# Sliding-window copy: loads moved to GpSimd's queue, four half-batch stores first, and half of the last unit stored by plain transfers

## The chip, the cores and the metric

One core of a Trainium2 chip. The metric is device time in microseconds (us), a median over runs; the granted clock was 1.0 in every run. A profiled execution is one of these; its own clock (the "span") starts a little later and ends a little earlier than the time that is scored, by 1.7 us in all (195.64 against 193.9).

## The reference

For a batch of 16 images of 64 channels and 64 x 64 pixels, every window of 8 x 8 at stride 4 is copied out.

```python
n_h = (h - window_size) // stride + 1      # 15
n_w = (w - window_size) // stride + 1      # 15
for i in range(n_h):
    for j in range(n_w):
        result[:, i, j] = x[:, :, i*4 : i*4 + 8, j*4 : j*4 + 8]
```

16.78 MB come in and 58.98 MB go out: 3600 rows (16 x 15 x 15) of 16 KB. There is no arithmetic on the data.

## The kernel before

The input stays in on-chip memory (L). A partition holds 32 of the 64 channels (bit 6 of its number says which) and a quarter of the picture rows of one image. VectorE and ScalarE gather windows from L into one of four staging tiles G, a window of 16 KB per partition, and an indirect store on GpSimd's queue scatters the 128 rows. An index beyond the output makes the store skip that row: of the 33 x 128 rows of all stores 624 have such an index, and the trace has 3600 packets of 16 KB, one for each of the other rows.

```python
SMALL = 4
for y in range(NY):                 # two half-batches
    for q in range(HQ):             # four quarters of the picture
        load(nc.sync, 0, y, q, SMALL, CL)      # 8 partitions, channels 4..31
        load(nc.gpsimd, 0, y, q, 0, SMALL)     # the same partitions, channels 0..3
        load(nc.gpsimd, 1, y, q, 0, CL)        # 8 partitions from 64 up, channels 32..63
...
EARLY = 3
for t in range(NG):                 # zero what a half-batch store reads but doesn't write
    ...
        nc.vector.memset(G[t][p0 : p0 + QP, :, :, :], 0.0)
for y in range(NY):
    for j in range(EARLY):          # half-batch stores: 64 rows
        ...
        scatter(G[t % NG], (idx_y0, idx_y1)[y], j, 0)
units = [(j, s) for j in range(NW) for s in (0, 2) if s or j >= EARLY]
for j, s in units:
    if s == 0:                      # "plain" unit: 128 rows
        ...
        scatter(g, idx, j, s)
    else:                           # "cross" unit: 112 rows
        turn = j % 2
        fill(g, turn, s, j, 0, HP, (act, act))
        fill(g, 1 - turn, s + 1, j, 0, HP, (dve, dve))
        scatter(g, (idx_hi, idx_lo)[turn], j, s)
```

A cross unit has 16 rows that don't exist. With idx_hi they are skipped in partitions 64 to 127, with idx_lo in partitions 0 to 63.

Of the kernel before, what the change touches and what calls it, by code (L numbers as in the profile page):

```python
# [1 line left out]

# [4 lines left out]


@with_exitstack  # L10
def kernel(
    ctx: ExitStack,
    tc: tile.TileContext,
    x: bass.AP,
    window_size: int,
    stride: int,
    out: bass.AP,
):
    nc = tc.nc
    P = nc.NUM_PARTITIONS  # L20

    B, C, H, W = x.shape
    Bo, NH, NW, Co, WSo, WSo2 = out.shape
    WS = int(window_size)
    ST = int(stride)
    assert Bo == B and Co == C and WSo == WS and WSo2 == WS

    f32 = mybir.dt.float32
    i32 = mybir.dt.int32
    ALU = mybir.AluOpType  # L30
    CH = 2
    HQ = P // (B * CH)
    CL = C // CH
    RB = H // HQ
    NSLOT = RB // ST
    NWIN = NH * NW
    CFREE = C * WS * WS
    HP = P // CH
    YB = 8
    NY = B // YB  # L40
    QP = YB * HQ
    assert HQ == 4 and WS == 2 * ST and QP == 32 and NSLOT == 4

    lpool = ctx.enter_context(tc.tile_pool(name="lpool", bufs=1))
    ipool = ctx.enter_context(tc.tile_pool(name="ipool", bufs=1))
    gpool = ctx.enter_context(tc.tile_pool(name="gpool", bufs=1))


    L = lpool.tile([P, CL, RB, W], f32)
    x_v = x.rearrange("(y b) (ch cl) (hq r) w -> ch y hq b cl (r w)", y=NY, ch=CH, hq=HQ)  # L50


    SMALL = 4

    def load(eng, ch, y, q, c0, c1):
        p0 = ch * HP + y * QP + q
        eng.dma_start(out=L[p0 : p0 + QP - HQ + 1 : HQ, c0:c1, :, :], in_=x_v[ch, y, q, :, c0:c1, :])  # L57



    def itile(name):
        return ipool.tile([P, 1], i32, name=name)

    pi, tb, tq, tc_, th, idx, idx_y0, idx_y1, idx_lo, idx_hi = (
        itile(n) for n in ("pi", "tb", "tq", "tc", "th", "idx", "idx_y0", "idx_y1", "idx_lo", "idx_hi")
    )
    FAR = float(2 * B * NWIN)
    nc.gpsimd.iota(pi[:, :], pattern=[[0, 1]], base=0, channel_multiplier=1)  # L68

    def bits(d, shift, mask):  # L70
        nc.vector.tensor_scalar(out=d[:, :], in0=pi[:, :], scalar1=shift, scalar2=mask, op0=ALU.logical_shift_right, op1=ALU.bitwise_and)

    def mul(d, a, m):
        nc.vector.tensor_scalar(out=d[:, :], in0=a[:, :], scalar1=float(m), scalar2=None, op0=ALU.mult)  # L74

    def tt(d, a, b, op):
        nc.vector.tensor_tensor(out=d[:, :], in0=a[:, :], in1=b[:, :], op=op)  # L77

    bits(tb, 2, B - 1)
    bits(tq, 0, HQ - 1)  # L80
    bits(tc_, 6, 1)
    mul(tb, tb, NWIN)
    mul(th, tq, NSLOT * NW)
    tt(tb, tb, th, ALU.add)
    mul(th, tc_, NW)
    tt(idx, tb, th, ALU.add)

    bits(th, 5, 1)
    mul(th, th, FAR)
    tt(idx_y0, idx, th, ALU.add)  # L90
    nc.vector.tensor_scalar(out=th[:, :], in0=th[:, :], scalar1=-1.0, scalar2=FAR, op0=ALU.mult, op1=ALU.add)  # L91
    tt(idx_y1, idx, th, ALU.add)

    nc.vector.tensor_scalar(out=tq[:, :], in0=tq[:, :], scalar1=float(HQ - 1), scalar2=FAR, op0=ALU.is_equal, op1=ALU.mult)
    tt(th, tc_, tq, ALU.mult)
    tt(idx_hi, idx, th, ALU.add)
    nc.vector.tensor_scalar(out=tc_[:, :], in0=tc_[:, :], scalar1=-1.0, scalar2=1.0, op0=ALU.mult, op1=ALU.add)
    tt(th, tc_, tq, ALU.mult)
    tt(idx_lo, tb, th, ALU.add)
    mul(th, tc_, NW)  # L100
    tt(idx_lo, idx_lo, th, ALU.add)

    for y in range(NY):
        for q in range(HQ):
            load(nc.sync, 0, y, q, SMALL, CL)
            load(nc.gpsimd, 0, y, q, 0, SMALL)
            load(nc.gpsimd, 1, y, q, 0, CL)

    o_v = out.rearrange("b i j c r w -> (b i j) (c r w)")
    nxt = [min(p + 1, 31) for p in range(32)]  # L110
    NG = 4
    G = [gpool.tile([P, C, WS, WS], f32, name=f"G{n}") for n in range(NG)]

    def scatter(g, ix, j, s):
        st = nc.gpsimd.indirect_dma_start(  # L115
            out=o_v,
            out_offset=bass.IndirectOffsetOnAxis(ap=ix[:, 0:1], axis=0),
            in_=g.rearrange("p c r w -> p (c r w)"),
            in_offset=None,
            element_offset=(s * NW + j) * CFREE,  # L120
            bounds_check=B * NWIN - 1,
            oob_is_err=False,
        )
        tc.declare_no_dep(st.ins, group="stores", reason="each store writes rows of its own")
        tc.add_to_no_dep_group("stores", st.ins)

    def fill(g, half, s, j, lo, n, copies):

        d = slice(half * HP + lo, half * HP + lo + n)
        cols = slice(j * ST, j * ST + WS)  # L130
        for ch in (half, 1 - half):
            f = slice(ch * HP + lo, ch * HP + lo + n)
            cs = slice(ch * CL, (ch + 1) * CL)
            copy = copies[ch != half]
            if s < NSLOT - 1:
                copy(out=g[d, cs, :, :], in_=L[f, :, s * ST : s * ST + WS, cols])  # L136
            else:
                copy(out=g[d, cs, 0:ST, :], in_=L[f, :, s * ST : RB, cols])  # L138
                nc.vector.stream_shuffle(out=g[d, cs, ST:WS, :], in_=L[f, :, 0:ST, cols], mask=nxt)  # L139

    act, dve = nc.scalar.copy, nc.vector.tensor_copy



    EARLY = 3
    assert EARLY < NG
    for t in range(NG):
        for half in range(CH):
            p0 = half * HP + (QP if t < EARLY else 0)
            nc.vector.memset(G[t][p0 : p0 + QP, :, :, :], 0.0)  # L150
    t = 0
    for y in range(NY):
        for j in range(EARLY):
            for half in range(CH):
                copies = (dve, dve) if y and half and j == 1 else (act, dve)
                fill(G[t % NG], half, half, j, y * QP, QP, copies)
            scatter(G[t % NG], (idx_y0, idx_y1)[y], j, 0)
            t += 1

    units = [(j, s) for j in range(NW) for s in (0, 2) if s or j >= EARLY]  # L160
    for j, s in units:
        g = G[t % NG]
        t += 1
        if s == 0:
            for half in range(CH):
                fill(g, half, s + half, j, 0, HP, (act, dve))
            scatter(g, idx, j, s)
        else:

            turn = j % 2  # L170
            fill(g, turn, s, j, 0, HP, (act, act))
            fill(g, 1 - turn, s + 1, j, 0, HP, (dve, dve))
            scatter(g, (idx_hi, idx_lo)[turn], j, s)


# [1 line left out]
_INS = ['x', 'window_size', 'stride']  # L177
_OUTS = [((16, 15, 15, 64, 8, 8), 'float32')]

_NUMBERS = {'window_size': 8, 'stride': 4}  # L180


# [26 lines left out]
```

## Time and profile before

| | before |
|---|---|
| time | 195.66 us (195.56 to 195.69, 3 runs) |
| span in the profile | 193.9 us |
| VectorE, ScalarE, GpSimd busy | 68%, 64%, 27% |
| last load landed | 47.5 us |
| first store issued | 44.5 us |
| last store landed, engines of partitions 64 to 127 / 0 to 63 | 187.8 / 190.4 us |
| middle duration of a 16 KB packet of a store | 618 ns |

The rows to read first are the DMA digits of the page (tenths of busy time in each of 40 slices) and the GB/s below them. Landing times and packet durations come from the trace's records of semaphore steps (a semaphore is the counter on which engines wait for a transfer; each store on GpSimd's queue steps its own 16 times) and of packets (the pieces of a transfer, each with a start, a duration and a size in the trace: 4 KB in the loads, 16 KB in the stores, and many of 4 bytes). All times count from the start of the span.

### The profile page before, as it was taken

To read this page: it belongs to the slowest core of one execution; us is meant where nothing else is said; L and a number is where in the kernel's file an instruction comes from. 1 tells how busy PE (TensorE), PEld (TensorE's weight loads), DVE (VectorE), ACT (ScalarE), POOL (GpSimd) and SP (SyncE) were. 2 spreads that over 40 slices of the span, in tenths; PEclk is the share of its full clock that TensorE was granted. 3 is DMA by queue.
4 is the path that set the end of the run, shared out by engine and by line. 5 is a ranking of instruction groups with operands and counts; after the bars stand their busy time and mean duration, and the time that the engine had idled before them with its cause. 6 is when DMAs were issued, how large, how long until landed. Compare 5 with 4: busy or idle time off the path is not lost.

```text
span 193.9 us, 478 instructions
## 1 busy us (share of the span) xinstructions
DVE 131.9 (68%) x156; ACT 123.5 (64%) x66; POOL 53.3 (27%) x54
## 2 busy tenths in 40 slices
DVE  6887778995999998766577657774777477643000
ACT  0000008960999999999779677977797779772000
POOL 7402211106463233231404211331323232311000
DMA  2999999999989999999999999999999999999980
GB/s 85 326 408 401 402 399 397 400 400 405 426 333 382 406 419 419 423 423 404 426 433 421 416 419 419 423 423 433 423 416 412 426 423 423 426 416 421 412 345 30
DMA packets 11476, 75.81 MB, mean 391 GB/s; under 512 B 3776, under 2 KB 3776, under 8 KB 7872
## 3 DMA queue, kind: packets, MB, share of 16 engines
q0 software_dynamic: 9616, 68.43, 85.9%
q1 hardware_dynamic: 1856, 7.34, 9.8%
q14 instruction: 4, 0.03, 0.0%
HBM read 16.78 MB, written 69.21 MB: 444 GB/s over the span
## 4 chain that ended last, share of the span: by engine, by line
DMA 66%; DVE 17%; issue 6%; POOL 2%; POOLq 1%; DVEq 0%; PEldq 0%
DMA out_dram<-G,idx 21%; DMA L<-in_x_dram 18%; DMA out_dram<-G,idx_hi 14%; DMA out_dram<-G,idx_lo 12%; DVE G L136 8%; DVE G L139 6%; DVE G L138 3%; POOL L L57 2%; POOLq L204 1%; DVEq L136 0%; POOL pi L68 0%; DVEq L138 0%; PEldq L204 0%
## 5 line engine op out<-in xcount | busy, mean ns | idle before, releaser
L136 ACT COPY G<-L 64x2048 f32<-64x2048 f32 (+1 forms) x65 | 122.2, 1896 | 22.5 <-DMA out_dram<-G,idx 9.9
L136 DVE COPY G<-L 64x2048 f32<-64x2048 f32 (+1 forms) x37 | 44.8, 1221 | 15.6 <-DMA out_dram<-G,idx 12.7
L139 DVE STREAM_SHUFFLE G<-L 64x1024 f32<-64x1024 f32 x30 | 38.3, 1275 | 0.0
L138 DVE COPY G<-L 64x1024 f32<-64x1024 f32 x30 | 20.7, 690 | 20.1 <-DMA out_dram<-G,idx_hi 13.3
L150 DVE MEMSET G<- 32x4096 f32 x8 | 27.8, 3472 | 7.9 <-issue 6.2
L115 POOL DMA_INDIRECT out_dram<-G,idx x12 | 12.4, 1030 | 33.3 <-ACT G L136 33.3
L115 POOL DMA_INDIRECT out_dram<-G,idx_hi x8 | 11.8, 1471 | 31.4 <-DVE G L139 17.8
L136 ACT ACT_TABLE_LOAD x1 | 1.3, 1283 | 29.6 <-DMA L<-in_x_dram 29.6
L57 POOL DMA_DIRECT2D L<-in_x_dram x16 | 9.8, 626 | 25.0 <-DMA L<-in_x_dram 24.4
L115 POOL DMA_INDIRECT out_dram<-G,idx_lo x7 | 9.7, 1390 | 20.5 <-ACT G L136 14.3
L115 POOL DMA_INDIRECT out_dram<-G,idx_y x6 | 9.3, 1547 | 13.7 <-DVE G L136 8.8
L77 DVE TENSOR_TENSOR th<-tc,tq 128x1 int32<-128x1 int32 x2 | 0.3, 159 | 0.1
L77 DVE CUSTOM_DVE_ANT_0 idx_y<-idx,th 128x2 uint16<-128x2 uint16 x2 | 0.3, 158 | 0.1
L74 DVE TENSOR_SCALAR th<-tc 128x1 int32<-128x1 int32 x2 | 0.3, 154 | 0.1
L68 POOL IOTA pi<- 128x1 int32 x1 | 0.1, 125 | 0.4 <-PEq L204 0.4
L139 DVE LOAD_MASK_SELECT G<-L x30 | 0.2, 6 | 0.0
L77 DVE CUSTOM_DVE_ANT_0 idx_hi<-idx,th 128x2 uint16<-128x2 uint16 x1 | 0.2, 159 | 0.0
L77 DVE CUSTOM_DVE_ANT_0 idx_lo<-tb,th 128x2 uint16<-128x2 uint16 x1 | 0.2, 159 | 0.0
L77 DVE CUSTOM_DVE_ANT_0 idx<-tb,th 128x2 uint16<-128x2 uint16 x1 | 0.2, 161 | 0.0
L77 DVE CUSTOM_DVE_ANT_0 idx_lo<-idx_lo,th 128x2 uint16<-128x2 uint16 x1 | 0.2, 158 | 0.0
L77 DVE CUSTOM_DVE_ANT_0 tb<-tb,th 128x2 uint16<-128x2 uint16 x1 | 0.2, 159 | 0.0
L91 DVE TENSOR_SCALAR th<-th 128x1 int32<-128x1 int32 x1 | 0.2, 153 | 0.0
(13 smaller groups left out, 1.7 us busy)
## 6 DMA issues: line engine op xcount, KB each, us to landing
L<-in_x_dram POOLq DMA_DIRECT2D x8, 1024.0 KB, 21.1
L<-in_x_dram SPq DMA_DIRECT2D x8, 896.0 KB
L<-in_x_dram POOLq DMA_DIRECT2D x8, 128.0 KB, 21.3
out_dram<-G,idx POOLq DMA_INDIRECT x12, 14.6
out_dram<-G,idx_hi POOLq DMA_INDIRECT x8, 13.9
out_dram<-G,idx_lo POOLq DMA_INDIRECT x7, 14.1
out_dram<-G,idx_y POOLq DMA_INDIRECT x6, 6.2
```

The costliest lines, as they stand in the source:

```text
L57: eng.dma_start(out=L[p0 : p0 + QP - HQ + 1 : HQ, c0:c1, :, :], in_=x_v[ch, y, q, :, c0:c1, :])
L68: nc.gpsimd.iota(pi[:, :], pattern=[[0, 1]], base=0, channel_multiplier=1)
L74: nc.vector.tensor_scalar(out=d[:, :], in0=a[:, :], scalar1=float(m), scalar2=None, op0=ALU.mult)
L77: nc.vector.tensor_tensor(out=d[:, :], in0=a[:, :], in1=b[:, :], op=op)
L91: nc.vector.tensor_scalar(out=th[:, :], in0=th[:, :], scalar1=-1.0, scalar2=FAR, op0=ALU.mult, op1=ALU.add)
L115: st = nc.gpsimd.indirect_dma_start(out=o_v, out_offset=bass.IndirectOffsetOnAxis(ap=ix[:, 0:1], axis=0), in_=g.rearrange("p c r w -> p (c ...
L136: copy(out=g[d, cs, :, :], in_=L[f, :, s * ST : s * ST + WS, cols])
L138: copy(out=g[d, cs, 0:ST, :], in_=L[f, :, s * ST : RB, cols])
L139: nc.vector.stream_shuffle(out=g[d, cs, ST:WS, :], in_=L[f, :, 0:ST, cols], mask=nxt)
L150: nc.vector.memset(G[t][p0 : p0 + QP, :, :, :], 0.0)
L204: with _tile.TileContext(nc) as tc:
```

## The change

Its intent: finish the first half-batch of loads sooner, have four stores ready when the loads end, take the zeroing off VectorE, and let the last transfers leave by a second queue.

```diff
-    SMALL = 4
+    SMALL, HWP = 4, 2
...
     for y in range(NY):
         for q in range(HQ):
-            load(nc.sync, 0, y, q, SMALL, CL)
-            load(nc.gpsimd, 0, y, q, 0, SMALL)
+            hw = y * HQ + q < HWP
+            if hw:
+                load(nc.sync, 0, y, q, SMALL, CL)
+            load(nc.gpsimd, 0, y, q, 0, SMALL if hw else CL)
             load(nc.gpsimd, 1, y, q, 0, CL)
...
-    EARLY = 3            # and eight memsets on VectorE
+    EARLY = NG
+    zero = ipool.tile([P, 1], f32, name="zero")
+    for g in G:
+        act(out=g.rearrange("p c r w -> p (c r w)"), in_=zero.to_broadcast([P, CFREE]))
...
+            if j == NW - 1:                      # the last unit, a plain one
+                scatter(g, idx_c1, j, s)         # its partitions 64 to 127
+                for y in range(NY):
+                    for q in range(HQ):          # its partitions 0 to 63
+                        free(nc.sync.dma_start(out=o_q[q * NSLOT + s, j, y], in_=g_q[y, q]))
+                return
...
-            turn = j % 2
+            turn = int(crossed % 5 in (1, 3))
...
+    for j in range(EARLY):
+        part(0, j)                               # four stores of the first half-batch
+    for j in range(EARLY):
+        part(1, j)
+        unit(*plain.pop(0))
+    unit(*cross.pop(0))
+    while plain:
+        unit(*cross.pop(0))
+        unit(*cross.pop(0))
+        unit(*plain.pop(0))
```

Two small tiles are new in the pool of index tiles, `idx_c1` and `zero`.

More of the change, by code (lines that the diff above doesn't have):

```diff
@@ L62, in itile @@
         return ipool.tile([P, 1], i32, name=name)
-    pi, tb, tq, tc_, th, idx, idx_y0, idx_y1, idx_lo, idx_hi = (
-        itile(n) for n in ("pi", "tb", "tq", "tc", "th", "idx", "idx_y0", "idx_y1", "idx_lo", "idx_hi")
+    pi, tb, tq, tc_, th, idx, idx_y0, idx_y1, idx_lo, idx_hi, idx_c1 = (
+        itile(n) for n in ("pi", "tb", "tq", "tc", "th", "idx", "idx_y0", "idx_y1", "idx_lo", "idx_hi", "idx_c1")
     )
@@ L99 @@
     tt(idx_lo, tb, th, ALU.add)
+    mul(th, tc_, FAR)
+    tt(idx_c1, idx, th, ALU.add)
     mul(th, tc_, NW)
@@ L112, with free @@
     G = [gpool.tile([P, C, WS, WS], f32, name=f"G{n}") for n in range(NG)]
+    o_q = out.rearrange("(y b) i j c r w -> i j y b (c r w)", y=NY)
+    def free(st):
+        tc.declare_no_dep(st.ins, group="stores", reason="each store writes rows of its own")
+        tc.add_to_no_dep_group("stores", st.ins)
     def scatter(g, ix, j, s):
@@ L123, in scatter @@
         )
-        tc.declare_no_dep(st.ins, group="stores", reason="each store writes rows of its own")
-        tc.add_to_no_dep_group("stores", st.ins)
+        free(st)
     def fill(g, half, s, j, lo, n, copies):
@@ L141, with tile_, part, unit @@
     act, dve = nc.scalar.copy, nc.vector.tensor_copy
-    EARLY = 3
-    assert EARLY < NG
-    for t in range(NG):
-        for half in range(CH):
-            p0 = half * HP + (QP if t < EARLY else 0)
-            nc.vector.memset(G[t][p0 : p0 + QP, :, :, :], 0.0)
-    t = 0
-    for y in range(NY):
-        for j in range(EARLY):
-            for half in range(CH):
-                copies = (dve, dve) if y and half and j == 1 else (act, dve)
-                fill(G[t % NG], half, half, j, y * QP, QP, copies)
-            scatter(G[t % NG], (idx_y0, idx_y1)[y], j, 0)
-            t += 1
-    units = [(j, s) for j in range(NW) for s in (0, 2) if s or j >= EARLY]
-    for j, s in units:
-        g = G[t % NG]
-        t += 1
+    EARLY = NG
+    zero = ipool.tile([P, 1], f32, name="zero")
+    nc.vector.memset(zero[:, :], 0.0)
+    for g in G:
+        act(out=g.rearrange("p c r w -> p (c r w)"), in_=zero.to_broadcast([P, CFREE]))
+    at = 0
+    def tile_():
+        nonlocal at
+        at += 1
+        return G[(at - 1) % NG]
+    def part(y, j):
+        g = tile_()
+        for half in range(CH):
+            fill(g, half, half, j, y * QP, QP, (dve, dve) if y and half else (act, dve))
+        scatter(g, (idx_y0, idx_y1)[y], j, 0)
+    crossed = 0
+    def unit(j, s):
+        nonlocal crossed
+        g = tile_()
         if s == 0:
             for half in range(CH):
-                fill(g, half, s + half, j, 0, HP, (act, dve))
+                fill(g, half, half, j, 0, HP, (act, dve))
+            if j == NW - 1:
+                scatter(g, idx_c1, j, s)
+                g_q = g[0:HP].rearrange("(y b q) c r w -> y q b (c r w)", y=NY, q=HQ)
+                for y in range(NY):
+                    for q in range(HQ):
+                        free(nc.sync.dma_start(out=o_q[q * NSLOT + s, j, y], in_=g_q[y, q]))
+                return
             scatter(g, idx, j, s)
         else:
-            turn = j % 2
+            turn = int(crossed % 5 in (1, 3))
+            crossed += 1
             fill(g, turn, s, j, 0, HP, (act, act))
@@ L173 @@
             scatter(g, (idx_hi, idx_lo)[turn], j, s)
+    for j in range(EARLY):
+        part(0, j)
+    plain = [(j, 0) for j in range(EARLY, NW)]
+    cross = [(j, 2) for j in range(NW)]
+    for j in range(EARLY):
[6 more added lines that the diff above has]
+        unit(*plain.pop(0))
 _INS = ['x', 'window_size', 'stride']
```

## The prediction

> **What bounds the kernel now.** I read, in this order, the page's DMA lines, a table of stretches, GpSimd's timeline, and then the landing events in the trace. First the page. The columns are 40 slices of 4.85 us.
>
> ```profile
> DVE  6887778995999998766577657774777477643000
> ACT  0000008960999999999779677977797779772000
> DMA  2999999999989999999999999999999999999980
> GB/s 85 326 408 401 402 399 397 400 400 405 426 333 382 406 419 419 423 423 404 426 433 421 416 419 419 423 423 433 423 416 412 426 423 423 426 416 421 412 345 30
> q0 software_dynamic: 9616, 68.43, 85.9%
> q1 hardware_dynamic: 1856, 7.34, 9.8%
> ```
>
> The DMA engines are busy nearly all the time, while VectorE (DVE) and ScalarE (ACT) are at 68% and 64%. So the kernel is bound by transfers: 16.78 MB in, 58.98 MB out, the sum of the two queues. No change of engine work can gain except where the DMA digits fall below 9: the start, slices 11 and 12, and the end. The table of stretches prices those (its last two columns are DMA share and GB/s):
>
> ```profile
> 5.00:10.00 5.00, 4.00 (x7) 0.00 (x0) 2.06 (x4) 1.00 0.99 333
> 10.00:46.00 36.00, 29.99 (x28) 12.27 (x7) 5.74 (x8) 1.00 1.04 399
> 54.00:58.00 4.00, 3.91 (x6) 3.95 (x3) 2.41 (x3) 1.00 0.82 330
> 58.00:68.00 10.00, 9.84 (x16) 9.88 (x6) 2.63 (x3) 1.00 0.93 385
> 68.00:184.00 116.00, 75.00 (x97) 91.47 (x49) 31.92 (x25) 1.00 1.01 421
> 187.00:190.00 3.00, 0.00 (x0) 0.00 (x0) 0.00 (x0) 1.00 0.43 180
> 190.00:194.00 4.00, 0.00 (x0) 0.00 (x0) 0.00 (x0) 1.00 0.00 0
> ```
>
> Loads run at 399 GB/s, stores at 421. The dip at 54 to 68 us is short of 421 by (421-330)x4 + (421-385)x10 = 724 KB, worth 1.7 us at most. From 187 to 190 us only 43% of the engines work, and then come nearly 4 us without any transfer. Why the dip is there, GpSimd's (POOL) timeline tells:
>
> ```profile
> 47.67 1.73 POOL L115 DMA_INDIRECT out_dram<-G,idx_y  x1 [0.30 <-issue]
> 52.10 2.20 POOL L115 DMA_INDIRECT out_dram<-G,idx_y  x1 [2.70 <-ACT G L136]
> 54.94 1.86 POOL L115 DMA_INDIRECT out_dram<-G,idx_y  x1 [0.65 <-issue]
> 57.74 0.96 POOL L115 DMA_INDIRECT out_dram<-G,idx_y  x1 [0.94 <-ACT G L136]
> 61.59 0.96 POOL L115 DMA_INDIRECT out_dram<-G,idx_hi  x1 [2.88 <-ACT G L136]
> ```
>
> The first three half-batch stores (64 rows of 16 KB, 2.5 us each) are in the queue when the loads end at 47.5 us, so they last until 55. The fourth is issued from 52.1 to 54.3 and its bytes begin about 1 us later. The filling engines were late: only three stores were ready.
>
> Last, the landings. Each store on GpSimd's queue steps its semaphore 16 times, in the trace as two groups of eight at two times. In the last store one group lands at 187.5 to 187.8 us, the other at 190.0 to 190.4 with one straggler at 191.0. The later group gains on the other by about 1.2 us with each idx_hi store (which skips 16 rows of partitions 64 to 127) and gives it back with each idx_lo store (which skips 16 rows of partitions 0 to 63). So the late group is the eight engines that carry partitions 0 to 63; I call them the low half, the others the high half. Between the 10th and the 32nd store they moved 1312 rows in 102.9 us, 164 per engine, 0.6274 us a row; the high half moved 1328 in 102.5 us, 0.6175 us a row. **The end is set by the low half**, which has more rows (1808 against 1792 in all) and is 1.6% slower.
>
> [...] 399 GB/s in 10 to 46 us, with SyncE's (SP) queue beside GpSimd's until 45.6 us, and no more. [...] each SP load of 8 partitions steps its semaphore once at issue and eight times at landing. Which eight is not shown directly, but the small GpSimd loads share SP's pace and the large ones don't, as if in alternate halves. [...] the scatter takes 0.96 us beside a shuffle (57.74) and 1.73 to 2.20 us beside copies (47.67, 52.10).
>
> **Part by part.** *Loads.* Six of SP's eight loads move to GpSimd's queue. Bytes and halves stay equal: the low half gets 2x28+2x4+6x32 = 256 packets of 4 KB per engine, the high half 8x32 = 256. [...] What changes is order: before, the two queues shared, and the first half-batch was complete only at about 36.4 us (ScalarE's wait for it ends there); now it is in order and should be there at about 26 us. Time of the low half: 64 packets by 14.7 us as before (the second SP load landed then), and 192 at 0.161 x 1.016 us (a 1 MB load of the high half took 5.15 us for 32) = 31.4, so 46.1 us in place of 47.5: the old tail of small loads behind SP goes. **-1.4 us.**
>
> *Zeroing.* Eight VectorE memsets (27.8 us) become four ScalarE copies of 4096 columns: 2 x 1.9 = 3.8 us each, 15 us, done by 18 us. The index arithmetic, which ended at 38.7 us between memsets, ends in the first few us. All beside loads, gain only through the next point.
>
> *Four first stores.* From 26 us ScalarE makes eight copies of 1.85 us: the four stores are ready at 35, 37, 39 and 41 us, all queued before the loads end at 46.1. They feed the engines for 4 x 2.5 = 10 us, to 56. The first tile is free at 48.6, refilled by three VectorE copies (3.7 us) at 52.4, issued by 54.4, moving by 55.4. The margin is 0.7 us. After that a half store and a full one (2.5 + 5.0 us of transfer) need VectorE 3.7 + 2.5 and ScalarE 1.9 + 3.8 us, less than 7.5, so the dip should go. In the low half the dip costs: 47.5 + 226 x 0.6274 = 189.3 against 190.2 seen. **-0.9 us.**
>
> *Rows.* The cross units go from 8 hi, 7 lo to 9 hi, 6 lo. The low half then has 8x32 + 11x64 + 9x64 + 6x48 = 1824 rows of 3600, two more per engine: 2 x 0.6274 = **+1.25 us.** The order of units costs nothing: two crosses and a plain need ScalarE 11.5 us and VectorE 10.3 of 13.6 us of transfer.
>
> *Last unit.* The scatter with the new index sends 64 rows from the high half, and eight SP transfers of 8 rows send the others. [...] The last tile is filled some 13 us of transfer before the end, so eight issues of at most 0.8 us (as SP's first two loads) are hidden. **0.**
>
> Sum: 46.1 + 228 x 0.6274 = 189.1 us for the low half in place of 190.2, and the same 3.7 us from there to the end: -1.1 us, so 194.6 from 195.66.
>
> **The rivals.** *SP's eight transfers spread over all 16 engines, or fall on the high half.* [...] for it, that 9 hi to 6 lo is an odd choice unless something relieves the low half. Spread, the low half has 1792 rows: 46.1 + 224 x 0.6274 = 186.6 us, -3.6, so 192.1. On the high half: 45 + 1840/8 x 0.6175 = 187.0, so 192.5. I give these two a quarter. *The refill does not keep up* after the four early stores (margin 0.7 us, and VectorE copies slow the issue): the dip comes back at 56 us, +1 us, 195.6. *One software queue loads more slowly than two*, or waits for one of its eight semaphores (a load waits for the landing of the one eight before it; 24.4 us of such waits now, none of which starved an engine): loads end at 48 or later, 196.5. *The whole dip and tail go* (1.7 + 2.5 us): 191.5; against it, the row counts.
>
> **Range and chances.** My sum says 194.6; the quarter for the first rival pulls it to 194.2. Low: that rival with a little more at the start. High: slow loads or the dip back. 191.8 to 196.4. Faster by over 2% needs 191.7, which takes the rival and luck: 0.12. Slower by over 2% needs 199.6, for which I see no mechanism: 0.02.
>
> **What would show it.** First store issued at about 35 us, not 44.5; no memset group; DMA digits all 9 in slices 11 and 12. Loads landed at about 46 us. At the end 5 to 6 us with about half of the engines busy, the sign of the uneven rows; if instead both halves end within 1 us, SP's transfers went elsewhere and the first rival holds. If the queue runs dry at 55 us or loads land after 47.5, those steps are wrong.

The sum is -1.1 us (loads -1.4, first stores -0.9, rows +1.25, last unit 0), so 194.6 us from 195.66, pulled to 194.2 by the first rival. Two zeros in it stand as estimates alone: that loads on one queue keep the bandwidth of two, and that SyncE's eight stores go to the low half, 8 rows per engine either way. What the trace had for the second was the eight steps at the landing of each of SyncE's loads.

## The result

196.56 us (196.49 to 196.58, 4 runs) against 195.61 us (195.48 to 195.69) of the kernel before in the same rounds: ratio 1.0049, 95% interval 1.0031 to 1.0066, so slower by half a per cent. A ratio here is the mean time of one kernel's runs over that of the other's of the same rounds, so not quite the ratio of the quoted medians. The prediction was 194.2 with a range up to 196.4.

The page of the changed kernel, the same lines as before (q0 is GpSimd's queue and q1 SyncE's: packets, MB, share of the 16 engines' time):

```profile
DVE  6000069300399997799695775795895774952000
ACT  8993069930389795999898787798797777954000
DMA  2999999999978999999999999999999999999950
GB/s 89 322 397 395 386 383 387 382 388 429 426 327 377 431 431 419 424 431 426 427 431 427 421 429 431 424 431 431 431 424 424 427 427 427 427 426 431 404 215 7
q0 software_dynamic: 12448, 72.90, 91.2%
q1 hardware_dynamic: 592, 2.88, 3.9%
```

VectorE is free in the first quarter as meant. But slices 2 to 8 (the loads) have 382 to 397 GB/s where 397 to 408 stood; slice 11 still has its dip (327 after 333); and the stores of the middle run mostly at 424 to 431 where mostly 416 to 426 stood. The table of stretches (busy time of three engines, clock, DMA share, GB/s):

```profile
10.00:46.00 36.00, 9.53 (x8) 20.73 (x10) 9.57 (x11) 1.00 1.04 390
54.00:58.00 4.00, 3.91 (x4) 3.58 (x2) 1.59 (x1) 1.00 0.82 344
58.00:68.00 10.00, 9.75 (x9) 8.84 (x6) 5.84 (x4) 1.00 0.95 398
68.00:180.00 112.00, 83.05 (x112) 91.91 (x49) 32.81 (x26) 1.00 1.01 426
184.00:187.00 3.00, 0.00 (x0) 0.00 (x0) 0.00 (x0) 1.00 0.59 251
187.00:190.00 3.00, 0.00 (x0) 0.00 (x0) 0.00 (x0) 1.00 0.53 219
```

Loads 390 for 399; the dip almost as deep; the middle faster, 426 for 421, which nothing in the prediction foresees; and from about 185 us on only half of the engines work, for 5 us in place of 2.5. GpSimd's timeline around the dip:

```profile
35.72 1.05 POOL L126 DMA_INDIRECT out_dram<-G,idx_y  x1 [6.68 <-ACT G L146]
...
41.09 0.96 POOL L126 DMA_INDIRECT out_dram<-G,idx_y  x1 [0.83 <-ACT G L146]
56.41 1.86 POOL L126 DMA_INDIRECT out_dram<-G,idx_y  x1 [14.35 <-ACT G L146]
```

The four early stores are issued at 35.7 to 41.1 us, as predicted (35 to 41), before the loads end. The fifth starts at 56.41, not by 54.4 at the latest: a hole of 14.35 us in the queue's supply. SyncE's plain transfers and the last scatter in the timeline of all engines:

```profile
175.71 10.57 SPq L187 DMA_DIRECT2D out_dram<-G  x8
177.88 0.96 POOL L126 DMA_INDIRECT out_dram<-G,idx_c  x1 [4.70 <-ACT G L146]
```

The eight issues take 10.57 us, 1.32 us each.

### The profile page after: what moved, and what is told of

It reads as the page before. It is cut to its first block, busy times and chain, and to the rows that moved or that the text cites. A ratio compares the mean times of both kernels' runs of the same rounds, so it can differ in the third digit from the quotient of the medians.

```text
span 194.8 us, 479 instructions
## 1 busy us (share of the span) xinstructions
DVE 111.4 (57%) x156; ACT 136.2 (70%) x69; POOL 56.0 (29%) x55
## 4 chain that ended last, share of the span: by engine, by line
DMA 66%; DVE 16%; issue 6%; POOL 2%; POOLq 1%; DVEq 0%; PEldq 0%
DMA out_dram<-G,idx_hi 35%; DMA out_dram<-G,idx 13%; DVE G L146 12%; DMA L<-in_x_dram 11%; DMA out_dram<-G,idx_y 8%; DVE G L149 3%; POOL L L58 2%; DVE G L148 2%; POOLq L240 1%; DVEq L146 0%; POOL pi L69 0%; POOLq L126 0%; DVEq L148 0%; PEldq L240 0%
## 5 line engine op out<-in xcount | busy, mean ns | idle before, releaser
L146 ACT COPY G<-L 64x2048 f32<-64x2048 f32 (+1 forms) x64 | 120.8, 1896 | 40.6 <-DMA out_dram<-G,idx_y 11.7
L146 DVE COPY G<-L 64x2048 f32<-64x2048 f32 (+1 forms) x42 | 51.2, 1231 | 44.9 <-DMA L<-in_x_dram 21.8
L126 POOL DMA_INDIRECT out_dram<-G,idx_y x8 | 12.0, 1495 | 29.1 <-ACT G L146 27.2
L58 POOL DMA_DIRECT2D L<-in_x_dram x16 | 11.5, 724 | 16.6 <-DMA L<-in_x_dram 15.9
L159 ACT COPY G<-zero 128x4096 f32<-128x4096 f32 x4 | 14.1, 3600 | 0.0
L126 POOL DMA_INDIRECT out_dram<-G,idx_lo x6 | 6.7, 1121 | 22.8 <-DVE G L149 11.9
L126 POOL DMA_INDIRECT out_dram<-G,idx_c x1 | 1.0, 962 | 4.7 <-ACT G L146 4.7
```

Of the source, the lines that this page charges most:

```text
L58: eng.dma_start(out=L[p0 : p0 + QP - HQ + 1 : HQ, c0:c1, :, :], in_=x_v[ch, y, q, :, c0:c1, :])
L126: st = nc.gpsimd.indirect_dma_start(out=o_v, out_offset=bass.IndirectOffsetOnAxis(ap=ix[:, 0:1], axis=0), in_=g.rearrange("p c r w -> p (c ...
L146: copy(out=g[d, cs, :, :], in_=L[f, :, s * ST : s * ST + WS, cols])
L159: act(out=g.rearrange("p c r w -> p (c r w)"), in_=zero.to_broadcast([P, CFREE]))
```

## The experiments

As in the prediction, the high half is the eight DMA engines that carry partitions 64 to 127 of a store, the low half those of partitions 0 to 63. The kernel before took 195.62 us in the rounds of e1 to e4 and 195.65 in those of the rest. All kernels computed the right result; each has four to six runs.

| run | us | ratio to before (95%) |
|---|---|---|
| changed kernel | 196.56 | 1.0049 (1.0031 to 1.0066) |
| e1 changed, 8 hi 7 lo | 195.44 | 0.9991 (0.9977 to 1.0005) |
| e2 changed, last unit by one scatter | 196.07 | 1.0025 (1.0012 to 1.0039) |
| e3 changed, loads of before | 194.93 | 0.9966 (0.9952 to 0.9980) |
| e4 before, changed loads | 196.92 | 1.0066 (1.0052 to 1.0080) |
| e5 before, two idle tiles | 194.00 | 0.9910 (0.9895 to 0.9925) |
| e6 changed, load order turned | 196.61 | 1.0044 (1.0030 to 1.0057) |
| e7 changed, SyncE loads channels 0 to 31 | 218.83 | 1.1181 (1.1166 to 1.1196) |
| e8 changed, L moved by 128 bytes | 195.00 | 0.9966 (0.9952 to 0.9979) |
| e9 early stores, zeroing, order alone | 193.64 | 0.9891 (0.9876 to 0.9906) |
| e10 best parts, two queues | 191.31 | 0.9776 (0.9763 to 0.9788) |
| e11 best parts, one queue | 192.40 | 0.9826 (0.9812 to 0.9839) |
| e12 changed, G moved by 192 bytes | 198.12 | 1.0124 (1.0109 to 1.0140) |

**e1: the rows.** From the changed kernel:

```diff
-            turn = int(crossed % 5 in (1, 3))
+            turn = j % 2
```

> The changed kernel with the cross units alternating again (8 hi, 7 lo in place of 9 and 6), all else as changed. Theory 1 (rows): the end is set by the low half (partitions 0 to 63), which carries 228 rows per engine in the changed kernel and landed at 190.3 us while the high half landed at 184.9; two rows fewer at 0.618 us each give -1.2 us: 195.3 us, and the gap between the halves at the end shrinks from 5.4 to about 2.9 us. Rival (the tail is made by SyncE's eight transfers, which need 10.6 us to issue): no change within 0.3 us, 196.3 to 196.6.

195.44 us, 1.1 us less. In the stretches, the end (columns as above):

```profile
184.00:187.00 3.00, 0.00 (x0) 0.00 (x0) 0.00 (x0) 1.00 0.82 350
187.00:190.00 3.00, 0.00 (x0) 0.00 (x0) 0.00 (x0) 1.00 0.35 142
```

The high half's last store landed at 186.5 us, in the changed kernel at 185.3, and the low half's last store landed at 190.8 in place of 191.9, both by the last step of the semaphore. The rows of the late half set the end.

**e2: the plain transfers.**

```diff
-            if j == NW - 1:
+            if False:
```

> The changed kernel with the last unit leaving by one scatter of all 128 rows, no SyncE stores. Theory 1 (rows): the same 8 rows per engine go through the low half either way, so within 0.3 us of the changed kernel, 196.3 to 196.9. Rival 1 (SyncE's transfers make the tail, issued every 1.4 us, with stragglers at 191.8 us): faster by 0.5 to 1.5 us, 195.1 to 196.0. Rival 2 [...]: slower by 0.5 us or more.

196.07 us, 0.5 us less than the changed kernel: a little outside my 0.3, at the edge of the first rival. But nearly half of it had arisen before the last unit: the fifth store had landed at 61.6 us here and at 61.8 there, the last at 191.4 and 191.9. e9 and e3 differ by the plain transfers and by e1's edit together, 1.29 us, which leaves 0.17 for the transfers. So they cost 0.2 to 0.5 us, the two intervals overlap, and the cause of so small a difference stays open. They land in the low half, as the prediction's 0 takes it: in the changed kernel the high half's last store landed at 185.3 us, and the last four of the eight transfers landed from 188.6 to 191.7, each with eight steps of its semaphore. The end is as uneven with them (251 and 219 GB/s from 184 to 187 and 187 to 190 us) as in e2, where one scatter carries these rows (257 and 202).

**e3 and e4: the loads.** e3 puts SyncE's eight loads back into the changed kernel, e4 puts the changed loads into the kernel before.

```diff
-    SMALL, HWP = 4, 2       # e3, from the changed kernel
+    SMALL, HWP = 4, 8
```

```diff
+            hw = y * HQ + q < 2     # e4, from the kernel before
+            if hw:
-            load(nc.sync, 0, y, q, SMALL, CL)
-            load(nc.gpsimd, 0, y, q, 0, SMALL)
+                load(nc.sync, 0, y, q, SMALL, CL)
+            load(nc.gpsimd, 0, y, q, 0, SMALL if hw else CL)
```

> The changed kernel with all eight loads of channels 4 to 31 on SyncE's queue, as in the kernel before. Theory 1: two queues load faster (5.15 us a load of 1 MB in the high half instead of 5.4), so the last load lands at 47.5 us instead of 49.4; but the first half-batch is complete only at 36 us, so the four early stores leave at 45 to 51 us instead of 36 to 41, and the dip stays. Net -0.5 us: 196.1, between 195.3 and 196.6. Rival (the loads' queue does not matter to the end): last landing and time as in the changed kernel, 196.5.

> The kernel before with nothing but the changed loads (two on SyncE, the rest on GpSimd's queue). Theory 1 (one software queue loads more slowly): the last load lands at 49.4 us instead of 47.5, the stores start no earlier because VectorE's memsets still end at 37 us, so +1 to +2 us: 196.6 to 197.6. Rival (the order of the loads helps, because the first half-batch is complete at 28 us instead of 36): 194.5 to 195.5.

e4: 196.92 us, 1.3 us more than before, inside what the theory expected. e3: 194.93 us, 1.6 us less than the changed kernel, in the theory's direction, but more than its 0.5 and below its range of 195.3 to 196.6. The stretch of the loads of e4:

```profile
10.00:46.00 36.00, 29.99 (x28) 12.27 (x7) 6.11 (x8) 1.00 1.04 389
```

and of e3:

```profile
10.00:46.00 36.00, 9.38 (x8) 20.73 (x10) 9.16 (x10) 1.00 1.04 399
```

So 389 or 390 GB/s goes with the one queue and 399 with two, in either kernel. The landings say where: a 1 MB load of the high half takes 5.4 us with one queue (seven of them from 11.7 to 49.4 us in the changed kernel) and 5.2 with two (11.4 to 47.5 us before). With one queue the low half gets its last load at 47.5 us and the high half at 49.4; with two both are done at 47.5 to 48. This deepens the dip as well: a staging tile is free only when both halves have stored it. In the changed kernel the first tile was free at 51.9 us (low half 50.1), its refill was issued from 56.4, and the low half, whose fourth store landed at 57.4, had nothing to do for 1.9 us (the fifth took 2.5 us and landed at 61.8). In e3 the first tile was free at 50.3, the fourth store landed at 57.3 and 57.6 in the two halves and the fifth at 60.3, so the hole was 0.5 us at most. That would explain why e3 gained more than I expected. (The stretches are too coarse for a hole of this size: from 54 to 58 us e3 has 398 GB/s and e9, with the same loads and early stores, 340, though their fifth stores landed at 60.3 and 60.4.)

**e5 and e12: the start address of the staging tiles.** After e1 to e4 one thing had no cause: a 16 KB packet of a store took 611 ns in the middle in the changed kernel, e1, e2 and e3, and 618 ns in the kernel before and e4. The built programs place the staging tiles at byte 147,904 of each partition in the kernel before (577 x 256 + 192) and at 147,968 (578 x 256) in the changed kernel, because its two new index tiles take 32 bytes each. In these six kernels the duration goes with the address, and nothing more was known of it: 618 ns is 1.1% more than 611. e5 and e12 test it.

```diff
     FAR = float(2 * B * NWIN)          # e5, from the kernel before; e12: range(6), from the changed kernel
+    for n in range(2):
+        itile(f"pad{n}")
```

> The kernel before with two idle index tiles more, so that the staging tiles start 64 bytes later in each partition (at a multiple of 256 bytes, as they happen to in the changed kernel, which has two index tiles more). Theory A (the start address sets the rate of the stores: a 16 KB packet of a store took 611 ns in the middle in the changed kernel and in e1 to e3, 618 in the kernel before and in e4, which has its addresses): the packets drop to 611 ns and the time by 226 rows x 0.008 us = 1.8 us, 193.8 us. Rival (the order of the units, cross and plain, sets that rate): 618 ns stay, 195.6 us.

> The changed kernel with six idle index tiles more, so that its staging tiles start 192 bytes past a multiple of 256, where those of the kernel before start. Theory A: the hidden gain of the changed kernel goes: packets of 618 ns, 198.2 us, ratio 1.013. Rival: the start address mattered in the kernel before only (through its order of units): 196.6 us.

Two idle tiles took 1.65 us off the kernel before, and six put 1.56 us on the changed one. The packets had 611 ns (e5) and 616 ns (e12) in the middle, and the stores' stretch says the same; e5:

```profile
68.00:180.00 112.00, 75.30 (x97) 91.47 (x49) 32.46 (x25) 1.00 1.01 427
```

and e12:

```profile
68.00:180.00 112.00, 82.54 (x112) 91.90 (x49) 31.21 (x26) 1.00 1.01 420
```

The rate goes with the address in both kernels; the order of the units does nothing to it. Why a packet takes longer from the one address than from the other the traces don't show, and only these two addresses modulo 256, 192 and 0, were run. So the changed kernel held a gain of 1.6 us that its diff doesn't speak of.

**e6: is it the neighbouring reads?**

```diff
-            load(nc.gpsimd, 1, y, q, 0, CL)
+            load(nc.gpsimd, 1, y, HQ - 1 - q, 0, CL)
```

> The changed kernel with the loads of channels 32 to 63 in the opposite order of quarter rows (3, 2, 1, 0 in each half-batch). The question is why a 1 MB load of the high half takes 5.4 us in the changed kernel and 5.15 in the kernel before. Theory Q (both halves of the engines are fed by one software queue): 5.4 us stay, last load at 49.4 us, 196.5 us. Rival L (the two halves read neighbouring addresses in lockstep): 5.15 us, last load at 47.5 us, 195.0 us.

196.61 us, and 389 GB/s over the loads' stretch: as the changed kernel. The rival falls.

The packets in the kept traces tell more. A load on GpSimd's queue brings one 4-byte packet for each 4 KB packet: that queue has 3712 packets of 4 bytes in the kernel before, which is 2304 (its 4 KB packets) + 624 (skipped rows) + 49 transfers x 16 (their steps), and 5264 in the changed kernel, which is 3648 + 816 + 50 x 16. SyncE's queue has 64 for its 8 loads of 224 packets, 8 a load, as many as a load's steps at landing, so none that go with the 4 KB packets. A small packet lasts 9 ns in the middle. By their order in the trace, the small packets of a load run on the eight engines that don't carry it. In the kernel before, from 10 to 46 us, 71% of the 2005 of them are followed after 5 to 7 ns by the start of a 4 KB packet of SyncE's (about 10% would be by chance), and by one of GpSimd's own no more often than by chance (17%). Each holds its engine for about 6 ns: that far apart they start when they come in a row, as 96% of them do in the changed kernel. So one queue has more of them to serve:

| loads, from 12 us to | 4-byte packets per 4 KB packet | engine time per 4 KB packet | mean 4 KB packet |
|---|---|---|---|
| before, two queues, 44 us | 0.51 | 163.6 ns | 164.7 ns |
| changed, one queue, 46 us | 1.04 | 168.5 ns | 166.6 ns |
| e10, two queues, 43 us | 0.51 | 158.3 ns | 159.0 ns |
| e11, one queue, 44 us | 1.06 | 161.9 ns | 159.4 ns |

(Engine time is the time of all 16 engines over the number of 4 KB packets; packets overlap by some 4 ns.) The extra small packets come to 3.2 of the 4.9 ns that one queue costs in the changed kernel, and to 3.3 of 3.6 ns in e11. They account for most of what one queue costs. This is a sum from traces: no run changed these packets alone.

**e7: SyncE loads all of channels 0 to 31.**

```diff
-            hw = y * HQ + q < HWP
-            if hw:
-                load(nc.sync, 0, y, q, SMALL, CL)
-            load(nc.gpsimd, 0, y, q, 0, SMALL if hw else CL)
+            load(nc.sync, 0, y, q, 0, CL)
             load(nc.gpsimd, 1, y, q, 0, CL)
```

> The changed kernel with all of channels 0 to 31 loaded by SyncE (eight loads of 1 MB) and all of channels 32 to 63 by GpSimd, no small loads. Theory: as with two queues before, 5.15 us a load, last landing at 47.3 us on both halves; and since GpSimd's queue now has 8 loads in place of 16 taking turns with SyncE's 8, the first half-batch is complete at about 26 us, so the four early stores leave at 36 to 41 us and there is no dip: faster than e3 by 0.3 us, 194.6. Rival: the first half-batch is late again and the time is e3's, 194.9, or the last loads come later because SyncE's queue is the slower one.

218.83 us: both theories fail by 24 us. Its page:

```profile
DMA  3999996556985549999999999999999999999961
GB/s 100 290 267 284 380 280 220 202 210 262 419 332 207 220 193 435 420 412 423 426 429 426 433 423 432 427 429 423 420 426 435 432 423 429 432 433 423 411 257 48
```

In slices 6 to 9 and 12 to 14 (counted from 0) about half of the engines work, at 193 to 262 GB/s. The trace of the kernel before tells how its loads lie on the halves. SyncE's second load steps its semaphore eight times at landing, at 13.9 to 14.7 us. A GpSimd load of 8 partitions has two groups of eight steps: the first large one at 11.0 to 11.4 and at 13.6 to 14.4 us, the small one after it at 11.2 to 11.6 and at 14.9 to 15.7. The large loads' first groups come 5.15 us apart, and the 4-byte packets, most of which belong to large loads (2048 of 2304, at one for each 4 KB packet), run beside SyncE's 4 KB packets (71%, under e6). So the large loads were on the half that SyncE doesn't use and the small ones on SyncE's: two halves in turn, in the order of issue. If that order alone decides, then without the small ones every second large load falls on SyncE's half: that half carries 8 + 4 MB, the other 4. The landings of e7 agree: one group of eight engines made its last step for a load at 35.0 us, the other at 72.2. Whatever the small loads were put there for, they keep the turns even.

**e8: the start address of the input tile.** L starts 128 bytes past a multiple of 256 in both kernels.

```diff
+    ppool = ctx.enter_context(tc.tile_pool(name="ppool", bufs=1))
+    for n in range(4):
+        ppool.tile([P, 1], i32, name=f"front{n}")
     lpool = ctx.enter_context(tc.tile_pool(name="lpool", bufs=1))
...                                       # and four idle index tiles, to keep G on a multiple of 256
```

> The changed kernel with the input tile moved 128 bytes up, to a multiple of 256 bytes as well (staging tiles stay on one). Theory A for writes: [...] last load at 48 us, 195.3 us. Rival (only reads of a store feel the start address): no change, 196.5 us.

The theory's gain per packet is cut from it: an estimate with no trace behind it, on which its 48 and 195.3 us rest.

195.00 us, 1.56 us less than the changed kernel. A 4 KB packet took 159 ns on nearly all occasions, where 159 to 172 had been usual; a 1 MB load took 5.2 us. The stretch of the loads:

```profile
10.00:46.00 36.00, 9.53 (x8) 20.73 (x10) 10.06 (x11) 1.00 1.05 408
```

**e9: early stores, zeroing and order alone.** This is e1's, e2's and e3's edit together on the changed kernel.

> The four early stores, the zeroing by ScalarE and the new order of units alone: the changed kernel with the loads of before, 8 hi and 7 lo, and one scatter for the last unit; staging tiles on a multiple of 256 bytes. To be read against e5 (the kernel before with the staging tiles moved, 194.0 us). Theory: the dip behind the loads shrinks (fourth store landed at 57.6 us and fifth at 60.3 in e3, against 57.8 to 58.3 and 60.4 to 61.3 in e5, and the ones after follow without gaps): e3 less 1.1 us for the rows (e1) less 0.5 us for the plain transfers (e2): 193.3 us, 0.7 us under e5. Rival: the early stores are hidden anyway, 194.0 us as e5.

193.64 us, against 194.00 of e5, which differs from it by just these parts: 0.4 us, half of what was expected, and the intervals of the two ratios overlap. In both the third store lands at 55.2 to 55.3 us; here the fourth follows at 57.8 and the fifth at 60.4, in e5 at 58.2 and 61.3 by the last of 16 steps, but at 57.9 and 60.5 by the 15th. So the holes that the early stores could fill were small.

**e10 and e11: the parts that help, together.** e10 is e9 with e8's edit and with `turn = 1 - j % 2` (7 hi, 8 lo). e11 is the same with the changed loads.

> A try at a version that beats both: e9 with the input tile on a multiple of 256 bytes too and 7 hi, 8 lo. Theory: loads of 5.1 us a MB, both halves end within 0.5 us of each other; e9 less 1.3 us (e8: start address of the input tile) less 1.2 us (two rows fewer per engine of the low half): 190.9 us. Rival: the high half becomes the late one and takes the gain of the rows back: 192.0 us.

> The same with the changed loads (two on SyncE, the rest on GpSimd's queue): the last 1 MB load lands at 47.4 us and the lower half's at 45.8, so the low half gets its stores earlier while the first tile comes free later. Theory (two queues are better): 0.5 to 1.5 us behind e10, 191.4 to 192.4. Rival (with the aligned input tile the single queue is no slower, 5.2 us a MB): within 0.3 us of e10.

(The 1.3 us that e10's theory takes for the input tile was an estimate; e8 measured 1.56.)

e10 took 191.31 us, 2.2% less than the kernel before and 2.7% less than the changed one by the medians, between the 190.9 and the 192.0 of its theory and its rival. Its stretches:

```profile
10.00:46.00 36.00, 9.38 (x8) 20.73 (x10) 9.64 (x11) 1.00 1.04 412
54.00:58.00 4.00, 3.91 (x4) 3.95 (x3) 3.36 (x2) 1.00 0.81 336
68.00:184.00 116.00, 80.08 (x110) 89.20 (x48) 32.45 (x26) 1.00 1.01 427
184.00:187.00 3.00, 0.00 (x0) 0.00 (x0) 0.00 (x0) 1.00 0.24 104
```

Loads at 412 GB/s, stores at 427, and both halves done together (last steps at 185.0 and 186.7 us). A dip is still there, 0.8 us at most by the landings (fourth store 55.9 and 56.6 us, fifth 59.2): the loads now end at 46.8 us, earlier than the refill can follow. e11 took 192.40, 1.1 us more, so one queue is slower with an aligned input tile too: 5.2 us for a 1 MB load against 5.0 in e10.

## Why the prediction was wrong

The changes measured one by one add up. The loads: +1.30 us (e4 against before). The rows: +1.12 (changed against e1). The plain transfers: +0.5 (changed against e2, with the doubt told there). Early stores, zeroing and order: -0.36 (e9 against e5). The start address: -1.65 (e5 against before). The sum is +0.9, and +0.95 was measured. So close a fit is in part luck: e3 puts the loads at 1.63, and with that the sum is +1.2.

*Loads, predicted -1.4 us.* This is the first step that failed. "192 at 0.161 x 1.016 us" took the pace of the high half from a profile with two queues and gave it to one queue that feeds both halves. The pace was 5.4 us for 1 MB in place of 5.15, the low half ended at 47.5 us instead of 46.1, and the high half, which I had given 45, ended at 49.4. In place of -1.4 the loads cost +1.3. The rival "One software queue loads more slowly than two" named this, but that its 196.5 us is nearly the measured time is luck: other errors and the start address below are in the measured time too. The order did what was meant (the first copies started at 26.2 us and the first store at 35.7). Why one queue is slower: reading neighbouring addresses together is excluded (e6), the start address is not the reason (e11 against e10), and the traces put 3.2 of 4.9 ns per 4 KB packet on the 4-byte packets that GpSimd's loads send through the other half (under e6). The prediction held that one queue gains no bandwidth (an estimate) and left out that it could cost some. Why the 4 KB packets, too, were 1.9 ns longer on average in the changed kernel stays open.

*Four first stores, predicted -0.9 us.* The stores were ready at the predicted times. The refill was not: "The first tile is free at 48.6" counted the low half alone. The tile was free at 51.9, after the slower half. The dip stayed, as in the rival "The refill does not keep up", with the low half idle for 1.9 us. With the loads of before (e9 against e5) the early stores, the zeroing and the order were worth 0.36 us, so 0.9 was too much even there.

*Rows, predicted +1.25 us.* Right: 1.12 in e1, and the 5 us of half-busy engines at the end were seen.

*Last unit, predicted 0.* Right in where the transfers go (an estimate then, measured under e2), a little short in cost: the issues took 1.32 us each and not at most 0.8, and 0.2 to 0.5 us were measured, of a cause that stays open. The rival that they spread over all engines falls.

*The term that was missing.* The sum held no gain from the start address of the staging tiles, which was -1.65 us. Without it the same errors would have stood out more: e12, the changed kernel with tiles placed as before, took 198.12 us, 1.2% over the kernel before. The two errors covered each other in part, so the miss of the range, 0.2 us, says less than the steps do. The order of instructions, which I had read, doesn't tell addresses; only the two added tiles hint at them.

## What to carry to other kernels

When transfers bound a kernel, read its DMA engines as groups and not as one pool: here a tile waits for the slower half (free at 51.9 us where the faster was done at 50.1), the end is set by the half with more rows (191.9 against 185.3 us in the changed kernel), an 8-partition load uses half of the engines (SyncE's step eight times at landing, GpSimd's in two groups of eight), on GpSimd's queue the two halves in turn as far as the traces tell (218.83 us when the turns were broken), and a load there sends small packets through the other half (one of 4 bytes for each 4 KB). Look at the start address of every tile that a transfer reads or writes: 64 bytes in front of a tile were worth 1.65 us of 195 (e5), more than anything the change was made for. And test the parts of a change one at a time, since a hidden gain can stand against a hidden loss.
